# A hybrid decoder layer on one core: the planner's prices, port rule and precedences set anew, and nine products of zeros on TensorE ahead of the first data

## The chip, the core and the metric

The kernel runs on one core of a Trainium2 chip. Five engines work side by side, each through its own list of instructions in a fixed order: TensorE (PE: products, into PSUM), VectorE (DVE), ScalarE (ACT), GpSimd (POOL) and SyncE (SP), which here issues the DMA transfers. An instruction that needs another engine's result waits for a semaphore, and everything behind it on its engine waits too. The metric is the device time of one execution in microseconds (us), lower is better.

## The reference

One step of a decoder layer over a prompt of 1024 tokens and 8 sample tokens, width 1024, all in four-byte floats. The input is projected to 9360 columns (16 of them a low-rank part of the GLA decay). These feed two branches: gated linear attention (GLA, 4 heads, a decay for each key column) and RWKV-7 (16 heads of 64, a delta rule with a 64x64 state). Both are gated, projected up, merged by sigmoid gates, projected out, and normed with the residual. Cut to its core:

```
p = x @ w_in
q, k, v, g_a, a_lr = split(p_gla);  log_a = log_sigmoid(a_lr @ w2 + b) / 16
o_gla = norm(gla_chunked(q, k, v, log_a, S0)) * silu(g_a)
pr = p_rwkv + (prev - p_rwkv) * mu;  r, kb, vb, g_b, w_lr, aa_lr = split(pr)
w = exp(-0.6065 * sigmoid(w0 + tanh(w_lr) @ w2));  a = sigmoid(a0 + aa_lr @ a2)
S_t = S_{t-1} (diag(w_t) - kk_t^T (kk_t * a_t)) + v_t^T k_t;  y_t = S_t r_t
o_rwkv = (groupnorm(y) + bonus) * silu(g_b)
m = sigmoid(gate_a) * (o_gla @ w_up_gla) + sigmoid(gate_b) * (o_rwkv @ w_up_rwkv)
y = layernorm(2**0.25 * x + m @ w_out)
```

The new GLA and RWKV states and the last projected RWKV rows are outputs too.

## The kernel before

**Tiling.** Activations are held transposed, 128 columns of the width on the partitions and tokens along the free dimension. The tokens are run in two passes: 520 (512 of the prompt and the 8 samples), in two tiles of 256 and 264, and then 512. Each of the 73 blocks of 128 output columns is a sum over 8 slabs of the width. To keep four-byte accuracy at TensorE's faster rate, weights and activations are split in a rounded high part and a low rest (`wpart`, `xh`, `xl`), and each slab takes three products: high by high, high by low, low by high. ScalarE makes the high parts (`high`), VectorE or GpSimd the low ones (`low`).

**The two branches.** A GLA head (`gla_head`) runs through seven levels of masked products in halves, then four chunks of 128 tokens. RWKV heads run in pairs (`pair`): `front` makes the scaled keys and queries (tiles `az`, `BK` and `L` in `wide`, `gg`) and solves the inside of each 64-token chunk in 32x32 blocks; the recursion for that (tiles `X`, `Xt`) is 62 small products on GpSimd for each pair. `back` joins the blocks: VectorE transposes `XT` into `Xt`, then TensorE multiplies. `turn` transposes on TensorE, with copies back into `wide`. `chain` carries the state through eight chunks, with a copy of PSUM after each of three products (`pch`), `norm` ends the pair. After the two passes come the up-projections and the output product with the layer norm.

**What sets the order.** Everything is written as generators that yield operations, each a stream. `Order.run` is a planner that runs when the kernel is built: it keeps a model time for each engine and, over and over, issues the ready operation with the lowest key. So the order of every engine's list follows from numbers at the top of the file:

- `price` (L149) gives the model duration of an operation.
[...]
[...]
- `PRIO` and `FOR_PE` are the precedences of the streams, off TensorE and on it; `STAND`, `SCARCE` and `PER_ROW` scale the latter; `URGENT` counts while no weights are ready; `LANDED`, `SWITCH`, `HOLD` and `TABLE` are delays of the model.
- `KEEP` is the number of row buffers that a projected block leaves to others; `EARLY_GATES` is how many saved gate rows are loaded ahead of the last gates of the second pass. With 8, which is their number in each loop, that wait is never reached.

The lines that decide between engines:

```
if eng in op.port:
    free = max(free, self.port["G" if eng == "V" else "V"])
...
end = t + cost
if len(op.ways) > 1:
    end += BIAS if eng == "V" and "A" in op.ways[0][0] else ASIDE if eng == "G" and "G" in op.port else 0.0
```

All operations of the streams are recorded at L221 in the profile, the line of the helper that calls them (L224 after the change), so the tiles tell them apart.

Of the kernel before, what the change touches and what calls it, by code (L numbers as in the profile page):

```python
# [10 lines left out]
F32 = mybir.dt.float32  # L11
# [9 lines left out]
P = 128  # L21
# [32 lines left out]
WBUF = {"wpart": ([P, 2, 512], 4), "wraw": ([P, 512], 3)}  # L54
BANKS = {"proj": 2, "big": 3, "pch": 1, "pY": 2}

KEEP = 3
AHEAD = 3

RAWS = 4  # L60


RANKW, RANKM = 48, 66
SPARE_ROWS = 7
EARLY_GATES = 5


HOP = {"P": 0.2, "D": 0.26, "G": 0.14, "V": 0.14, "A": 0.14}

SWITCH = 0.09  # L70
HOLD = 0.11
TABLE = 1.28

AGE = 0.5

SPARE = 0.4
LANDED = 0.5
BIAS = 0.104
ASIDE = 0.5

PRIO = {"evacuate": 0.7, "pair": 0.3, "turn": 0.5, "chain": 0.5, "norm": 0.1, "x": 0.65, "lora": -0.02, "rank":
        -0.15, "head": 0.3, "gate": -0.18, "w": 0.3, "out": 0.07, "state": 0.16, "block": 0.09}
FOR_PE = {"pair": 1.0, "turn": 1.0, "chain": 1.0, "norm": 1.0, "lora": 1.0, "rank": 1.0, "head": 1.0, "gate": 1.0,
        "state": 1.0, "out": -0.6}
STAND, SCARCE, PER_ROW = 0.017, 0.2, 0.03

URGENT = 0.6
SIGMOID, EXP = "sigmoid_and_others", "natural_log_exp_and_others"
SETS = {AF.Sigmoid: SIGMOID, AF.Tanh: SIGMOID, AF.Exp: EXP, AF.Ln: EXP}

# [14 lines left out]
CST_W = _o  # L105
# [43 lines left out]
def price(eng, name, out, args, ins):  # L149

    n = out.free_size()
    src = [x for x in ins if x.tensor.space != PSUM] if eng == "A" else ins
    if eng == "P":
        m = args[0].free_size()
        rows, cols = tiles(name, args)
        if name == "transpose":
            return 0.112
        if args[0].dtype == F32R:
            return max(m / 1200, n / 2165) if rows == cols == P else (m + n) / 1200
        if rows == cols == P:  # L160
            return 2 * max(m, n) / 1200 + 0.005
        return 2 * (max(m, n) if cols == P else m + n) / 1200 * rows * cols / P ** 2 + (0.01 if cols == P else 0.0)
    if eng == "S":
        return 0.56
    if eng == "A":
        extra = len(ins) - 1
        return 0.097 + n / 1200 + (0.042 if len(src) == len(ins) else 0.0) + 0.094 * extra
    wide = max([n, *(x.free_size() for x in ins)]) if name in ("tensor_reduce", "bn_stats", "bn_aggr") else n
    if eng == "V":
        if name == "tensor_tensor_scan":  # L170
            return 0.1 + n / 480
        if name in ("tensor_copy", "copy", "memset") and ins and ins[0].tensor.space != PSUM:
            wide = wide / 2
        scalars = sum(x.free_size() == 1 for x in ins[1:]) if name in ("scalar_tensor_tensor", "tensor_scalar") else 0
        return 0.068 + wide / (480 if name == "copy_predicated" else 960) + 0.06 * scalars
    if name in ("tensor_scalar", "memset"):
        return 0.08 + n / 760
    return 0.1 + n / (300 if name == "tensor_copy" else 456)


def shared(eng, name, out, ins):

    sb = [x for x in ins if x.tensor.space != PSUM and x.free_size() > 1]
    if eng == "G":
        return bool(sb)
    if name in ("tensor_copy", "copy"):
        return len(sb) > 0 and out.tensor.space != PSUM
    return name in ("tensor_mul", "tensor_add", "tensor_sub", "scalar_tensor_tensor") and len(sb) > 1


# [63 lines left out]
class Order:  # L254
# [83 lines left out]
    def start(self, op):  # L338

        best = None  # L340
        for eng, fn, cost in op.ways:
            free, t = self.time[eng] + (SWITCH if eng == "P" and op.tiles != self.tiles else 0.0), 0.0
            for x in (*op.outs, *op.ins):
# [81 lines left out]
class Kern(Order):  # L425
# [71 lines left out]
    def setup(self):  # L497
        nc, a = self.nc, self.a
        E = mybir.EngineType
        self.es.enter_context(self.tc.manual_schedule(engines={E.PE, E.Activation, E.DVE, E.Pool, E.SP}))  # L500
        cp = self.pool("const")
        wp = self.pool("w", side="left")
        self.dr = self.pool("dr", space=DRAM)
        pp = self.pool("psum", space=PSUM)
        xp = self.pool("x", side="right")
        self.r1 = r1 = self.pool("work", side="left")
        for tag, bufs in BANKS.items():
            self.buffers(tag, bufs, lambda tag=tag, bufs=bufs: pp.tile([P, 512], F32, name=tag, bufs=bufs))
        for tag, (shape, bufs) in SBUF.items():
            dt = F32R if tag in PARTS else F32  # L510
            self.buffers(tag, bufs, lambda tag=tag, shape=shape, bufs=bufs, dt=dt:
                         r1.tile(shape, dt, name=tag, bufs=bufs))
        for tag, (shape, bufs) in WBUF.items():
            dt = F32 if tag == "wraw" else F32R
            self.buffers(tag, bufs, lambda tag=tag, shape=shape, bufs=bufs, dt=dt:
                         wp.tile(shape, dt, name=tag, bufs=bufs))
        for k in range(NK):
            for v in "hl":
                tag = f"x{v}{k}"
                self.buffers(tag, 1, lambda tag=tag: xp.tile([P, HALF], F32R, name=tag, bufs=1))  # L520
        nc.scalar.preload_act_table_set(EXP)
        self.cons = cp.tile([P, CST_W], F32, name="cons")
        self.pv = cp.tile([P, PV_W], F32, name="pv")
        self.ident = self.cst("ident")
        self.omu = cp.tile([P, NRC], F32, name="omu")
        self.oka = cp.tile([P, 8], F32, name="oka")
        self.nkk = cp.tile([P, 8], F32, name="nkk")
        self.bias = {}
        for n, v in [("glaeps", GLA_EPS), ("gneps", GN_EPS), ("lneps", LN_EPS), ("one", 1.0),
                     ("kkl", 0.5 * math.log(KK_SCALE))]:  # L530
            t = cp.tile([P, 1], F32, name="b_" + n)
            nc.vector.memset(t, v)
            self.bias[n] = t
        dbg = getattr(self, "dbg", {})
        self.o_gla = dbg.get("o_gla", None) or self.dr.tile([D, T], F32, name="o_gla")
        self.o_rwkv = dbg.get("o_rwkv", None) or self.dr.tile([D, T], F32, name="o_rwkv")
        self.sg = [[[self.dr.tile([P, PASS[i][1]], F32, name=f"sg{i}{n}{k}") for k in range(NK)] for n in range(2)]
                   for i in range(2)]
        self.mg = [[self.dr.tile([P, PASS[i][1]], F32, name=f"mg{i}{k}") for k in range(NK)] for i in range(2)]

        self.lev = cp.tile([P, 2 * P * MASKED], U8, name="lev")

        self.onesr = cp.tile([P, P], F32R, name="onesr")
        self.headsr = cp.tile([P, P], F32R, name="headsr")
        self.wa = cp.tile([P, NK * RANKW + RANKM - RANKW], F32R, name="wa")
        self.alr = cp.tile([96, HALF], F32R, name="alr")
        self.gw2 = cp.tile([96, GH * GDK], F32R, name="gw2")

        self.GS = [self.dr.tile([P, GDV], F32, name=f"GS{h}") for h in range(GH)]
        self.Sp = [self.dr.tile([P, C], F32, name=f"Sp{n}") for n in range(NPAIR)]  # L550

        self.smp = cp.tile([P, 4, NPAIR, NS], F32, name="smp")
        self.RS = self.dr.tile([4, NS, D], F32, name="RS")
        self.WA = self.dr.tile([2, NS, D], F32, name="WA")
        self.tail = cp.tile([P, NS + 1, NRC], F32, name="tail")
        self.carry = cp.tile([P, NRC], F32, name="carry")
        self.shT = cp.tile([P, NRC, NS], F32, name="shT")
        self.reset = cp.tile([P, HT], U8, name="reset")
        nc.vector.memset(self.reset, 1)
        nc.vector.memset(self.reset[:, ::C], 0)  # L560


        for tag, n, bufs in (("az", 4 * HT, 2), ("XT", 2 * HT, 2), ("L1", HT, 1), ("As", HT, 1)):
            ts = [cp.tile([P, n], F32, name=f"{tag}{i}") for i in range(bufs)]
            for t in ts:
                nc.gpsimd.memset(t, 0.0)
            self.fixed(tag, ts)
# [244 lines left out]
    def gla_row(self, c, rows, scale, paired=None):  # L812
        x = yield from self.row(c.n, KEEP)
        rows.append(x)
# [658 lines left out]
    def gate_row(self, c, n, x):  # L1473
        gt = yield from self.row(c.n, KEEP)

# [313 lines left out]
```

## Time and profile before

| what | value |
|---|---|
| median of 3 runs | 1540.86 us (1540.79 to 1543.17) |
| the profiled execution's own time | 1540.08 us |
| its span, first to last instruction | 1538.3 us |
| granted TensorE clock, mean | 0.997 |
| idle time of TensorE in the span | 29.1 us |
| share of DMA engines in use | 64.8% |

The busy share of TensorE is high from the first weights on: of 31 stretches of 50 us, 28 have it busy for over 48 us. A row of the groups reads: line, engine, operation, output tile <- input tiles, shape, count, then busy time and the mean of one in ns, then the idle time before it with what ended it. A row of the timeline reads: start and length in us, engine, operation, tiles, count, with idle time before it in brackets. A row of the windows reads: stretch, its length, then busy time and count of PE, PEld, DVE, ACT and POOL, the granted clock, the DMA share and GB/s.

### The profile page before, as it was taken

To read this page: it belongs to the slowest core of one execution; us is meant where nothing else is said; L and a number is where in the kernel's file an instruction comes from. 1 tells how busy PE (TensorE), PEld (TensorE's weight loads), DVE (VectorE), ACT (ScalarE), POOL (GpSimd) and SP (SyncE) were. 2 spreads that over 40 slices of the span, in tenths; PEclk is the share of its full clock that TensorE was granted. 3 is DMA by queue.
4 is the path that set the end of the run, shared out by engine and by line. 5 is a ranking of instruction groups with operands and counts; after the bars stand their busy time and mean duration, and the time that the engine had idled before them with its cause. 6 is when DMAs were issued, how large, how long until landed. Compare 5 with 4: busy or idle time off the path is not lost.

```text
span 1538.3 us, 29435 instructions
## 1 busy us (share of the span) xinstructions
PE 1509.2 (98%) x10082; PEld 1347.0 (88%) x10082; DVE 1108.5 (72%) x2324; ACT 837.6 (54%) x2021; POOL 478.1 (31%) x1228
## 2 busy tenths in 40 slices
PE   8999999999999999999999999999999999999998
PEld 8899999999999998888887878787888898897786
DVE  6677687867877796867657796879686856666565
ACT  5556766766566666655545463546556545554210
POOL 1060525042330825073523625451634050000000
PEclk9999999999999999999999999999999999999999
DMA  8777876788568874674565465636574676797432
GB/s 286 266 260 239 269 238 220 225 267 288 192 210 270 280 246 148 215 207 124 161 184 168 122 189 176 179 122 179 178 243 117 222 221 219 265 307 248 137 111 82
DMA packets 206641, 318.44 MB, mean 207 GB/s; under 512 B 87075, under 2 KB 102572, under 8 KB 206492
## 3 DMA queue, kind: packets, MB, share of 16 engines
q1 hardware_dynamic: 206492, 316.56, 64.8%
q8 instruction: 80, 1.31, 0.4%
q14 instruction: 69, 0.57, 0.1%
HBM read 196.82 MB, written 118.61 MB: 205 GB/s over the span
## 4 chain that ended last, share of the span: by engine, by line
PE 79%; DVE 9%; POOL 3%; DMA 3%; issue 2%; ACT 2%; SPq 1%; POOLq 0%; DVEq 0%; ACTq 0%
PE proj L221 47%; PE big L221 19%; PE pY L221 8%; PE pch L221 5%; DVE row L221 4%; POOL X L221 1%; POOL Xt L221 1%; SPq L221 1%; DVE az L221 1%; ACT row L221 1%; DVE part L221 1%; DMA row<-o_gla 1%; DVE wide L221 1%; DVE gg L221 1%; DVE xl L221 1%
## 5 line engine op out<-in xcount | busy, mean ns | idle before, releaser
L221 PE MATMUL proj<-xh,wpart 128*128 128x256 f32 (+2 forms) x3728 | 918.0, 329 | 6.0 <-ACT wpart L221 5.0
L221 PEld LDWEIGHTS proj<-xh,wpart 128*128 128x128 f32 x3728 | 622.8, 189 | 54.5 <-ACT wpart L221 5.0
L221 PE MATMUL proj<-xl,wpart 128*128 128x256 f32 (+2 forms) x1864 | 613.4, 329 | 0.4 <-DVE xl L221 0.4
L221 PEld LDWEIGHTS proj<-xl,wpart 128*128 128x128 f32 x1864 | 352.4, 189 | 21.8 <-DVE xl L221 1.2
L221 POOL TENSOR_TENSOR Xt<-X,wide 128x60 f32<-128x60 f32 (+24 forms) x496 | 166.3, 335 | 223.1 <-DMA wide<-LD 46.5
L221 DVE TENSOR_TENSOR wpart<-wraw,wpart 128x512 fp32r<-128x512 f32 x205 | 143.0, 699 | 70.0 <-ACT wpart L221 64.8
L221 POOL TENSOR_TENSOR X<-X,Xt 128x60 f32<-128x60 f32 (+24 forms) x496 | 172.6, 348 | 38.6
L221 ACT CAST wpart<-wraw 128x512 fp32r<-128x512 f32 x210 | 130.6, 623 | 86.1 <-PE proj L221 41.5
L221 DVE TENSOR_TENSOR row<-row 128x512 f32<-128x512 f32 (+9 forms) x292 | 158.3, 552 | 14.8 <-ACT row L221 8.0
L221 ACT ACTIVATE row<-row 128x512 f32<-128x512 f32 (+3 forms) x229 | 138.2, 611 | 36.0 <-DVE row L221 22.0
L221 POOL TENSOR_TENSOR row<-row 128x256 f32<-128x256 f32 (+6 forms) x77 | 73.3, 957 | 260.4 <-DVE row L221 105.6
L221 ACT ACTIVATE s0p<-wide,pc 64x64 f32<-64x64 f32 x256 | 88.2, 345 | 42.6 <-DVE wide L221 34.4
L221 ACT ACTIVATE row<-proj,omu 128x256 f32<-128x256 f32 (+1 forms) x97 | 53.2, 549 | 86.4 <-PE proj L221 84.5
L221 DVE SCALAR_TENSOR_TENSOR wide<-pch,pc,s0p 64x64 f32<-64x64 f32 x224 | 63.1, 282 | 37.4 <-PE pch L221 32.6
L221 POOL TENSOR_SCALAR XT<-XT,st 128x256 f32<-128x256 f32 x1 | 1.2, 1225 | 272.2 <-ACT st L221 272.2
L221 PE MATMUL big<-row 128*128 128x128 f32 (+3 forms) x456 | 84.2, 314 | 0.0
L221 DVE SCALAR_TENSOR_TENSOR row<-proj,pv,row 128x255 f32<-128x255 f32 (+1 forms) x97 | 55.4, 571 | 29.1 <-ACT tail L221 15.1
L221 PE MATMUL big<-xh,wpart 128*128 128x512 f32 (+2 forms) x304 | 73.3, 325 | 0.0
L221 ACT COPY wide<-pch 64x64 f32<-64x64 f32 x132 | 27.3, 207 | 75.8 <-PE pch L221 51.8
L221 ACT COPY row<-big 128x128 f32<-128x128 f32 (+7 forms) x130 | 39.1, 336 | 53.6 <-PE big L221 49.5
L221 DVE COPY rh<-pch 128x128 f32<-128x128 f32 x128 | 37.1, 290 | 41.8 <-PE pch L221 40.1
L221 ACT ACTIVATE row<-proj 128x128 f32<-128x128 f32 (+4 forms) x136 | 37.2, 326 | 50.9 <-PE proj L221 50.2
(250 smaller groups left out, 2635.5 us busy)
## 6 DMA issues: line engine op xcount, KB each, us to landing
w<-wpart SPq DMA_DIRECT2D x146, 512.0 KB
wpart<-w SPq DMA_DIRECT2D x146, 512.0 KB
wraw<-w_in SPq DMA_DIRECT2D x146, 256.0 KB
wide<-LD SPq DMA_DIRECT2D x64, 128.0 KB
wraw<-w_up_gla SPq DMA_DIRECT2D x32, 256.0 KB
wraw<-w_up_rwkv SPq DMA_DIRECT2D x32, 256.0 KB
sg<-row SPq DMA_DIRECT2D x16, 260.0 KB
row<-sg SPq DMA_DIRECT2D x16, 260.0 KB
```

The lines of the kernel that those rows point to most:

```text
L221: ways.append((eng, lambda call=call: call(out, *args, **kw), price(eng, name, out, args, ins)))
```

## The change

[...] No computation of the layer is changed. The zeros go to the PSUM bank `pch`, whose first later product overwrites them.

```
-KEEP = 3
+KEEP = 2
...
+WARM = 9
-EARLY_GATES = 5
+EARLY_GATES = 8
-SWITCH = 0.09
+SWITCH = 0.074
-LANDED = 0.5
-BIAS = 0.104
-ASIDE = 0.5
+LANDED = 0.605
+BIAS = 0.145
+ASIDE = 1.145
-PRIO = {... "x": 0.65, "lora": -0.02, ... "out": 0.07, ...}
+PRIO = {... "x": 0.56, "lora": 0.08, ... "out": -0.01, ...}
-FOR_PE = {"pair": 1.0, "turn": 1.0, "chain": 1.0, "norm": 1.0, "lora": 1.0, ... "out": -0.6}
+FOR_PE = {"pair": 1.0, "turn": 1.11, "chain": 1.0, "norm": 0.76, "lora": 0.41, ... "out": 0.05}
-STAND, SCARCE, PER_ROW = 0.017, 0.2, 0.03
+STAND, SCARCE, PER_ROW = 0.042, 0.2, 0.036
-URGENT = 0.6
+URGENT = 0.767
...
-            return 0.112
+            return 0.1095
         if args[0].dtype == F32R:
-            return max(m / 1200, n / 2165) if rows == cols == P else (m + n) / 1200
+            return max(m / 1200, 0.0045 + n / 2256) if rows == cols == P else (m + n) / 1200
...
-        extra = len(ins) - 1
+        extra = 0.5 * (len(ins) - 1) if src != ins else len(ins) - 1
...
+    if name in ("tensor_tensor_scan", "tensor_scalar"):
+        return out.free_size() > P and len(sb) > 0
...
+        warm, self.cons = cp.tile([P, P], F32, name="warm"), cp.tile([P, CST_W], F32, name="cons")
+        nc.vector.memset(warm, 0.0)
+        idle = pp.tile([P, 512], F32, name="pch", bufs=BANKS["pch"])
+        for n in range(WARM):
+            nc.tensor.matmul(idle[:, :P], warm, warm, start=True, stop=True)
```

What the numbers do is seen in the engines' lists. TensorE at the very start of the program, before the change (`xh`, `xl` are the first slab's high and low parts):

```order
L1785 UNCONDITIONAL_BRANCH
L221 MATMUL proj<-xh_191,wpart 128x256
L221 MATMUL proj<-xl_196,wpart 128x256
L221 MATMUL proj<-xh_191,wpart 128x256
L221 MATMUL proj<-xh_191,wpart 128x264
```

The same place after it:

```order
L1792 UNCONDITIONAL_BRANCH
L529 MATMUL pch<-warm 128x128 x9
L224 MATMUL proj<-xh_203,wpart 128x256
L224 MATMUL proj<-xl_208,wpart 128x256
L224 MATMUL proj<-xh_203,wpart 128x256
L224 MATMUL proj<-xh_203,wpart 128x264
```

The nine products stand ahead of the first slab; the products behind them are the same.

VectorE early in the first pass, before the change, from the third slab's low part on (`xl_249` is the fifth slab's, `wpart` are halves of weights, `onesr`, `alr` and `wa` are small constants and weights):

```order
L221 TENSOR_TENSOR xl_231<-row,xh_215 128x520
L221 TENSOR_TENSOR xl_242<-row,xh_230 128x520
L221 TENSOR_TENSOR xl_249<-row,xh_241 128x520
L221 MEMSET row 128x520
L221 TENSOR_TENSOR wpart<-wraw,wpart 128x512
L221 CAST onesr<-row 128x128
L221 MEMSET row 128x520
L221 TENSOR_TENSOR wpart<-wraw,wpart 128x512
L221 CAST alr<-row 96x520
L221 CAST wa<-row 128x402
L221 TENSOR_TENSOR xl_304<-row,xh_248 128x520
```

After it (`xl_262` is the fifth slab's):

```order
L224 TENSOR_TENSOR xl_245<-row,xh_227 128x520
L224 TENSOR_TENSOR xl_254<-row,xh_244 128x520
L224 MEMSET row 128x520
L224 CAST onesr<-row 128x128
L224 MEMSET row 128x520
L224 TENSOR_TENSOR wpart<-wraw,wpart 128x512
L224 CAST alr<-row 96x520
L224 CAST wa<-row 128x402
L224 TENSOR_TENSOR wpart<-wraw,wpart 128x512
L224 TENSOR_TENSOR xl_262<-row,xh_253 128x520
L224 TENSOR_TENSOR xl_319<-row,xh_261 128x520
```

The fifth slab's low part has moved behind two halves of weights and the small casts.

GpSimd between the recursions of the last pair of the first pass and the first pair of the second, before the change (`az` and `wide` are the pair's scaled operands, the products on `row` with three dimensions belong to the levels of a GLA head):

```order
L221 MEMSET row 128x8
L221 TENSOR_TENSOR row<-row 128x32x2x4 x2
L221 TENSOR_TENSOR row<-row 128x64
L221 TENSOR_TENSOR az_167<-row 64x8x64 x2
L221 COPY pc<-row 128x8
L221 TENSOR_TENSOR wide<-row 64x8x64
L221 TENSOR_TENSOR row<-row 128x4x2x32 x2
L221 TENSOR_TENSOR row<-row 128x8
L221 MEMSET wide 64x64 x2
L221 TENSOR_TENSOR row<-row 128x2x2x64 x2
L221 TENSOR_TENSOR row<-row 128x512
L221 MEMSET X 128x256
```

After it:

```order
L224 MEMSET row 128x8
L224 TENSOR_TENSOR wide<-row 64x8x64
L224 TENSOR_TENSOR row<-row 128x128x2 x2
L224 TENSOR_TENSOR row<-row 128x64x2x2
L224 TENSOR_TENSOR row<-row 128x128
L224 TENSOR_TENSOR row<-row 128x32x2x4 x2
L224 TENSOR_TENSOR row<-row 128x64
L224 MEMSET X 128x256
```

The two products into `az` and one of 512 columns on `row` are gone from GpSimd, that into `wide` is still there, and some smaller ones of the GLA head have come. Over the whole program, GpSimd's products of 512 or 520 columns (on `row`, `part`, `az`, `wpart` and `wide`) go from 56 to 12, and of the chain's 256 copies `wide<-pch` VectorE keeps 36 of 124 and ScalarE does 220 instead of 132.

More of the change, by code (lines that the diff above doesn't have):

```diff
@@ L76 @@
 SPARE = 0.4
-LANDED = 0.5
-BIAS = 0.104
-ASIDE = 0.5
[L81 to L84, printed above, removed]
-STAND, SCARCE, PER_ROW = 0.017, 0.2, 0.03
-URGENT = 0.6
+LANDED = 0.605
+BIAS = 0.145
+ASIDE = 1.145
+PRIO = {"evacuate": 0.7, "pair": 0.3, "turn": 0.5, "chain": 0.5, "norm": 0.1, "x": 0.56, "lora": 0.08, "rank":
+        -0.15, "head": 0.3, "gate": -0.18, "w": 0.3, "out": -0.01, "state": 0.16, "block": 0.09}
+FOR_PE = {"pair": 1.0, "turn": 1.11, "chain": 1.0, "norm": 0.76, "lora": 0.41, "rank": 1.0, "head": 1.0, "gate": 1.0,
+        "state": 1.0, "out": 0.05}
+STAND, SCARCE, PER_ROW = 0.042, 0.2, 0.036
+URGENT = 0.767
 SIGMOID, EXP = "sigmoid_and_others", "natural_log_exp_and_others"
@@ L156, in price @@
         if name == "transpose":
-            return 0.112
+            return 0.1095
         if args[0].dtype == F32R:
-            return max(m / 1200, n / 2165) if rows == cols == P else (m + n) / 1200
+            return max(m / 1200, 0.0045 + n / 2256) if rows == cols == P else (m + n) / 1200
         if rows == cols == P:
-            return 2 * max(m, n) / 1200 + 0.005
-        return 2 * (max(m, n) if cols == P else m + n) / 1200 * rows * cols / P ** 2 + (0.01 if cols == P else 0.0)
+            return 2 * max(m, n) / 1200 + 0.009
+        return 0.1365 if cols == P else 0.142 if rows == P else 0.95
     if eng == "S":
@@ L521, in setup @@
         nc.scalar.preload_act_table_set(EXP)
-        self.cons = cp.tile([P, CST_W], F32, name="cons")
+        warm, self.cons = cp.tile([P, P], F32, name="warm"), cp.tile([P, CST_W], F32, name="cons")
[3 more added lines that the diff above has]
+            nc.tensor.matmul(idle[:, :P], warm, warm, start=True, stop=True)
         self.pv = cp.tile([P, PV_W], F32, name="pv")
```

## The prediction

> **What bounds the kernel now.** I read the page first, then the waits of TensorE, then the timeline around the longest of them, then the groups of GpSimd.
>
> ```profile
> PE 1509.2 (98%) x10082; PEld 1347.0 (88%) x10082; DVE 1108.5 (72%) x2324; ACT 837.6 (54%) x2021; POOL 478.1 (31%) x1228
> ```
>
> TensorE is busy for 1509.2 of 1538.3 us. The change leaves its products as they are, apart from nine more, so only the 29 us in which it is idle, and stretches at a lower clock, can be won. The waits of TensorE say what that idle time is made of (us in total, times, longest):
>
> ```profile
> PE proj L221 <- ACT wpart L221: 5.0, 1, 5.0
> PE big L221 <- DVE part L221: 3.5, 7, 1.0
> PE big L221 <- DVE Xt L221: 3.4, 4, 1.7
> PE big L221 <- DVE wide L221: 2.0, 1, 2.0
> PE pch L221 <- DVE rh L221: 1.2, 3, 0.7
> PE proj L221 <- DVE row L221: 1.0, 1, 1.0
> ```
>
> ```profile
> 1530.72 0.43 DVE XT L221
> ```
>
> The first 5.0 us are the wait for the first weights. VectorE, though it is idle for 28% of the span, ends nearly all later waits: these five rows of it hold 11.1 us. The last products end at 1530.7 (the row of the chain that ended last), and the 7.6 us behind them hold steps that the change leaves alone. So the question is why VectorE is late at those few places. Two of them:
>
> ```profile
> 625.21 0.68 DVE L221 TENSOR_TENSOR az<-row 64x512 f32<-64x512 f32 x1
> ...
> 694.67 3.26 POOL L221 TENSOR_TENSOR az<-row 64x512 f32<-64x512 f32 x2 [1.46 <-DVE row L221]
> 698.63 1.60 POOL L221 TENSOR_TENSOR wide<-row 64x512 f32<-64x512 f32 x1
> 696.91 1.57 DVE L221 SCALAR_TENSOR_TENSOR row<-row 128x512 f32<-128x512 f32 x1
> 699.01 1.76 DVE L221 TENSOR_TENSOR az<-row 64x512 f32<-64x512 f32 x1
> 700.70 1.24 DVE L221 STREAM_TRANSPOSE Xt<-XT 32x128 f32<-32x128 f32 x4
> 702.00 1.08 PE L221 MATMUL big<-Xt,L 128*128 128x32 f32 x8 [1.70 <-DVE Xt L221]
> ...
> 983.34 2.83 POOL L221 TENSOR_TENSOR row<-row 128x512 f32<-128x512 f32 x2 [10.38 <-DMA row<-state_rwkv]
> 983.59 3.11 DVE L221 COPY gg<-az 64x512 f32<-64x512 f32 x2
> 907.11 0.85 DVE L221 COPY gg<-az 64x512 f32<-64x512 f32 x2
> 987.47 0.66 PE L221 MATMUL big<-cons,row 128*128 128x128 f32 x4 [1.99 <-DVE wide L221]
> ```
>
> The same product of 64x512 takes VectorE 0.68 us at 625.21 and 1.76 us at 699.01, where GpSimd runs a wide product of its own; the two copies into `gg` take 0.85 us alone (907.11) and 3.11 us beside GpSimd (983.59). Each time TensorE waits 1.7 to 2.0 us right behind; the second time for the copy into `wide`, which stands behind those into `gg`. What makes VectorE late is wide work on GpSimd at the same moment.
>
> **The change, part by part.** Its own time is 1540.08 us in the profiled execution (span 1538.3 and 1.8 around it), 0.05% below the median of 1540.86; the sum is made against 1540.08.
>
> (1) Wide products leave GpSimd. `ASIDE` more than doubles, and the port list grows. What GpSimd ran of 512 columns and more:
>
> ```profile
> L221 POOL TENSOR_TENSOR row<-row 128x512 f32<-128x512 f32 x23 | 32.3, 1408 | 113.3 <-DVE row L221 54.7 <-DMA row<-state_rwkv 26.5 <-ACT row L221 17.3
> L221 POOL TENSOR_TENSOR part<-row,part 128x512 fp32r<-128x512 f32 x12 | 17.1, 1429 | 71.9 <-ACT part L221 31.9 <-DVE part L221 28.8 <-PE big L221 11.2
> L221 POOL TENSOR_TENSOR row<-row 128x520 f32<-128x520 f32 x7 | 9.8, 1396 | 39.1 <-ACT row L221 39.1
> L221 POOL TENSOR_TENSOR az<-row 64x512 f32<-64x512 f32 x6 | 8.3, 1388 | 23.5 <-ACT row L221 13.6 <-issue 8.4 <-DVE row L221 1.5
> L221 POOL TENSOR_TENSOR wpart<-wraw,wpart 128x512 fp32r<-128x512 f32 x5 | 6.7, 1343 | 123.9 <-DMA wide<-LD 73.3 <-PE proj L221 25.9 <-ACT wpart L221 24.8
> L221 POOL TENSOR_TENSOR wide<-row 64x512 f32<-64x512 f32 x3 | 4.5, 1501 | 19.7 <-DVE row L221 19.6
> ```
>
> That is 56; the changed order leaves 12 of these kinds on GpSimd, none of `part` and none of `az`. The waits I lay to such meetings are those on `part`, `Xt` and `wide`, 3.5 + 3.4 + 2.0 = 8.9 us. After the wait of 1.70 us there is a price on top:
>
> ```profile
> 703.94 0.63 PE L221 MATMUL proj<-xl,wpart 128*128 128x512 f32 x1
> 703.23 0.39 PE L221 MATMUL proj<-xl,wpart 128*128 128x512 f32 x1
> 704.00:707.40 3.40, 3.40 (x14) 2.94 (x12) 3.35 (x8) 0.18 (x1) 0.00 (x0) 0.52 0.13 10
> ```
>
> The granted clock is 0.52 for 3.4 us, and a 512-column product takes 0.63 instead of 0.39. Five such products at 0.43 instead of 0.23 us from start to start cost 1.0 us. So 9.9 us hang on it. With 12 of the 56 left I take three quarters, **-7.4 us**; the bounds are 0 (each wait is dealt out anew elsewhere) and -12.1 (all 11.1 us of waits on VectorE and the clock).
>
> (2) The price of that: 44 products more on VectorE, 0.68 us each, 30 us. It gets back the chain's copies:
>
> ```profile
> L221 DVE COPY wide<-pch 64x64 f32<-64x64 f32 x124 | 27.4, 221 | 50.0 <-PE pch L221 45.8 <-ACT sto L221 1.1 <-ACT row L221 1.0
> L221 ACT COPY wide<-pch 64x64 f32<-64x64 f32 x132 | 27.3, 207 | 75.8 <-PE pch L221 51.8 <-DVE wide L221 22.2
> ```
>
> 88 of the 124 go to ScalarE, which is no slower at them (207 against 221 ns) and busy for 54%; VectorE loses 19 us. With some 0.9 us saved at each meeting that no longer happens, VectorE's busy time stays near 1108. In a stretch where it is fuller than on average, TensorE still does not wait:
>
> ```profile
> 200.00:250.00 50.00, 50.00 (x426) 49.13 (x425) 43.38 (x93) 33.62 (x94) 14.56 (x35) 1.00 0.71 228
> ```
>
> VectorE is busy for 43.38 of 50 us and TensorE for all 50. So most of the 44 are covered. But some now stand ahead of a step that TensorE waits for: I take **+2 us**, three or four of 0.6 us; the bounds are 0 and, with no cover at all, +30.
>
> (3) The nine products of zeros. Before:
>
> ```profile
> 7.58 0.58 PE L221 MATMUL pY<-xh,wpart 128*128 128x256 f32 x1 [0.58 <-ACT wpart L221]
> 8.31 0.80 PE L221 MATMUL pY<-xh,wpart 128*128 128x256 f32 x2
> 10.86 0.34 PE L221 MATMUL pY<-xl,wpart 128*128 128x256 f32 x1
> 11.40 0.28 PE L221 MATMUL pY<-xh,wpart 128*128 128x264 f32 x1
> 11.52 0.28 PE L221 MATMUL proj<-xh,wpart 128*128 128x256 f32 x1
> 8.36 2.04 DVE L221 TENSOR_TENSOR xl<-row,xh 128x520 fp32r<-128x520 f32 x3
> 10.46 0.49 DVE L221 MEMSET row<- 128x520 f32 x1
> 13.36 0.69 DVE L221 TENSOR_TENSOR xl<-row,xh 128x520 fp32r<-128x520 f32 x1
> ```
>
> From 8.31 to 10.86 eleven products start 0.23 us apart; from 11.40 on it is 0.12. At full pace these eleven take 1.3 instead of 2.55 us. Up to 8.3 the pace does not matter, since TensorE waits for weights there (7.58). Zeros can start once VectorE has cleared their tile, near 1.2 us (an estimate), and are 18 passes. The row at 702.00 holds eight such passes of four products, 1.08 us with the drain of the last, some 0.11 us each; at half the clock 18 of them are 4 us, and they end near 5.1, where the first real product starts (5.02). Then VectorE must keep up: the fifth slab's low part now stands behind two weight halves and the small casts. Those took 10.46 to 13.36 before; from 9.7, when two low parts are done, they end at 12.6, and that slab is ready at 13.3. TensorE wants it near 13.2. So -1.25 + 0.1 = **-1.1 us**; the bounds are +0.3 (no faster clock, and the zeros in the way) and -1.3.
>
> [...]
>
> (4) Other numbers (`KEEP`, `EARLY_GATES`, prices, precedences) move products among each other. The number of changes between full-rate and four-byte products on TensorE grows by some 45; at these changes the first starts later by what the last started earlier, so I take +0.5 in all, bounds -2 and +3.
>
> Sum: -7.4 + 2 - 1.1 + 0.5 = -6.0, and 1540.08 - 6.0 = **1534.1 us**.
>
> **Rivals.**
> (a) *All waits on VectorE shrink*, since the whole order fits better: -12.1 - 1.1 and no price, 1527. For it: nearly every row of waits names VectorE. Against: 12 wide products stay on GpSimd.
>
> (b) *Waits are only dealt anew.* Every engine has an order of its own, and moving 44 products shifts when all others come; the lost waits return on other rows. Then only the zeros and +0.5 remain: 1539.5. For it: 98% leaves little, and the waits are few and scattered.
>
> (c) *Slower: VectorE as the bound in front of the transposes into `Xt`.* The 44 products are 2.75 for each of 16 head pairs; inline, at some 0.61 us from start to start (0.68 less the overlap of two), they put those transposes, and the product that waits for them, 1.7 us later. Where TensorE has nothing else, it pays. Against the 8.0 us won by (1), (3) and (4) it decides from five pairs on; with nine it gives 1540.1 - 8.0 + 15.3 = 1547.4. Against it: the stretch with 43.38 above.
>
> (d) *The zeros wake nothing*: term (3) is 0 to +0.3, 1535.3.
>
> [...]
>
> ```profile
> L221 POOL TENSOR_TENSOR Xt<-X,wide 128x60 f32<-128x60 f32 (+24 forms) x496 | 166.3, 335 | 223.1 <-DMA wide<-LD 46.5
> ```
>
> **How the numbers follow.** The forecast as it stands 0.39, (d) 0.12, (a) 0.17, (b) 0.20, (c) 0.12. A measurement of this kernel tells about 0.2%, 3.1 us, from no change: faster is below 1537.8, slower above 1543.9. The forecast, (d) and (a) make 0.68, all faster but for 0.02 of (d) that lies above 1537.8: 0.66; (b) and that part 0.22; slower 0.12. The range goes from a little below (a), for waits that the rows above leave out, to the near end of (c): 1526 to 1543.
>
> **What would show it.** Right: GpSimd's wide groups at 12 in all, `gg` copies and `az` products at their undisturbed length, no wait over 1.5 us on `Xt` or `wide`, no half clock in mid-span, 0.12 us pace from 8.3 us on, VectorE's busy time near 1108. Wrong: `part` and `Xt` still lead the waits with more than 6 us together, or new rows of VectorE or ScalarE carry as much.

## The result, and the profile after

| | before | after |
|---|---|---|
| median | 1540.82 us (1540.38 to 1543.17) | 1521.02 us (1520.08 to 1524.11) |
| ratio, 95% interval | | 0.9872 (0.9855 to 0.9889) |
| profiled execution, its span | 1540.08, 1538.3 us | 1520.7, 1518.9 us |
| granted clock, mean | 0.997 | 0.999 |

The kernel is 1.28% faster, 19.8 us where 6.0 were forecast: the right direction, but below the range's lower end of 1526. From the page of the changed kernel, busy time, share of the span and instructions:

```profile
PE 1502.7 (99%) x10100; PEld 1348.3 (89%) x10100; DVE 1092.3 (72%) x2306; ACT 853.0 (56%) x2107; POOL 395.1 (26%) x1161
```

And TensorE's waits (us in total, times, longest):

```profile
PE big L224 <- issue: 1.7, 1, 1.7
PE pch L529 <- DVE warm L526: 1.0, 1, 1.0
PE proj L224 <- DVE row L224: 1.0, 1, 1.0
...
PE big L224 <- DVE part L224: 0.6, 2, 0.3
PE pch L224 <- DVE rh L224: 0.6, 1, 0.6
```

The waits on `part` fell from 3.5 to 0.6 us, those on `wide` are gone, and of `Xt` one is left (the first row, see below). Where the time went is seen by stage. The rows of the windows give stretch and length, then busy time of PE, PEld, DVE, ACT and POOL with counts, clock, DMA share and GB/s. Before:

```profile
50.00:600.00 550.00, 547.13 (x4535) 529.34 (x4534) 417.43 (x899) 351.23 (x922) 203.33 (x516) 1.00 0.75 242
600.00:1200.00 600.00, 590.32 (x3313) 491.64 (x3311) 446.32 (x962) 323.66 (x769) 242.62 (x627) 1.00 0.57 170
1200.00:1420.00 220.00, 217.65 (x1417) 195.25 (x1416) 144.02 (x283) 115.07 (x226) 21.71 (x66) 1.00 0.78 251
```

And after:

```profile
50.00:600.00 550.00, 549.12 (x4565) 531.75 (x4564) 418.66 (x914) 355.94 (x953) 177.28 (x504) 1.00 0.73 243
600.00:1200.00 600.00, 597.37 (x3404) 503.78 (x3403) 446.92 (x970) 345.34 (x848) 186.47 (x575) 1.00 0.59 180
1200.00:1420.00 220.00, 217.57 (x1372) 194.17 (x1371) 136.12 (x254) 111.90 (x214) 20.89 (x62) 1.00 0.75 240
```

From 600 to 1200 us, most of the second pass, TensorE starts 91 more products in the same time. That stage is where most of the gain is; from 1200 on nothing is won.

Idle time understates it: a product is still busy when the next one starts (0.28 us long, 0.12 us from start to start, for 264 columns), so a product that comes late by less than this overlap leaves no gap. So I also took **lateness** from the trace: the distance from one product's start to the next, less the median distance of the same form of product in the trace of before, summed by stage, in us (so products packed more tightly than the median count below zero). "Met" counts VectorE's instructions that took over 0.1 us longer than the undisturbed median of their form while GpSimd worked on something other than the recursion. "Chain" is where the last product of the last head pair's chain starts. Each row is one profiled execution, and stretches at half clock count in its lateness (13.7 us of half clock in the second pass of nudge_before, 20.5 us from 1200 to 1400 in port_alone and in nudge_after3). Behind 1400 another 3.2 us stand in port_alone, 7.2 in precedences_undone and 8.2 in nudge_after3, and under 1 in the others. The experiments stand in the table too:

| kernel | ratio to before | 0-50 | 50-600 | 600-1200 | 1200-1400 | met | chain |
|---|---|---|---|---|---|---|---|
| before | 1 | 5.1 | 8.7 | 15.7 | 4.5 | 48 | 1332 |
| **after** | 0.9872 | 4.0 | 4.1 | 0.8 | 5.7 | 12 | 1316 |
| zeros_alone | 0.9991 | 5.2 | 10.7 | 16.3 | 4.2 | 49 | 1334 |
| port_alone | 1.0114 | 4.5 | 10.5 | 9.4 | 23.2 | 21 | 1370 |
| moved | 1.0003 | 4.5 | 9.8 | 15.8 | 5.1 | 9 | 1333 |
| nudge_before | 1.0004 | 5.0 | 9.0 | 20.7 | 5.6 | 43 | 1338 |
| nudge_before2 | 1.0016 | 5.4 | 9.4 | 15.6 | 5.7 | 48 | 1329 |
| port_undone | 1.0013 | 5.1 | 12.7 | 15.3 | 8.7 | 47 | 1350 |
| aside_back | 1.0003 | 4.3 | 11.7 | 13.7 | 5.7 | 43 | 1320 |
| rule_out | 1.0043 | 3.8 | 18.3 | 7.0 | 13.9 | 22 | 1361 |
| prices_undone | 0.9965 | 6.7 | 6.4 | 8.4 | 12.5 | 18 | 1327 |
| precedences_undone | 1.0025 | 3.5 | 5.3 | 10.4 | 12.7 | 19 | 1354 |
| buffers_undone | 0.9946 | 3.9 | 9.8 | 8.3 | 4.8 | 11 | 1324 |
| zeros_undone | 0.9892 | 5.2 | 4.3 | 1.2 | 7.3 | 13 | 1320 |
| back | 0.9935 | 4.2 | 4.8 | 5.4 | 12.5 | 37 | 1328 |
| nudge_after | 0.9906 | 3.8 | 3.9 | 1.4 | 10.6 | 13 | 1311 |
| nudge_after2 | 0.9883 | 4.8 | 5.0 | 3.8 | 7.7 | 14 | 1322 |
| nudge_after3 | 1.0107 | 5.3 | 5.6 | 7.0 | 29.2 | 14 | 1369 |

From before to after the lateness falls by 19.3 us, from 34.0 to 14.7, which is the difference of the spans but for 0.1. Behind waits that the profile shows it falls by 12.3 (23.3 to 11.0, of which rows of idle time show 16.5 and 7.5); the start gives 1.3; the half-clock stretch of before 1.5 (the prediction's 1.0 for five products leaves out the short ones behind them); the other 4.2 are products that come closer without any wait shown.

Two places that the prediction named. The start after the change:

```profile
1.04 4.21 PE L529 MATMUL pch<-warm 128*128 128x128 f32 x18 [1.04 <-DVE warm L526]
4.91 0.58 PE L224 MATMUL proj<-xh,wpart 128*128 128x256 f32 x1
...
8.44 0.29 PE L224 MATMUL pY<-xh,wpart 128*128 128x264 f32 x1
8.57 0.28 PE L224 MATMUL proj<-xh,wpart 128*128 128x256 f32 x1
...
22.56 0.28 PE L224 MATMUL big<-xl,wa 128*66 128x264 f32 x1
```

```profile
23.81 0.28 PE L221 MATMUL big<-xl,wa 128*66 128x264 f32 x1
```

Products start 0.13 us apart at 8.44, and the one that started at 23.81 before (second fence) starts at 22.56: 1.25 us, as forecast. The other place is the wait for `Xt`, from the timeline after the change:

```profile
679.07 1.58 POOL L224 TENSOR_TENSOR wide<-row 64x512 f32<-64x512 f32 x1 [10.97 <-DVE row L224]
679.42 3.05 DVE L224 TENSOR_TENSOR az<-row 64x512 f32<-64x512 f32 x2
685.13 0.92 DVE L224 STREAM_TRANSPOSE Xt<-XT 32x128 f32<-32x128 f32 x3
686.47 1.05 PE L224 MATMUL big<-Xt,L 128*128 128x32 f32 x8 [1.70 <-issue]
```

And the window behind it, in the columns of the windows above:

```profile
686.40:689.80 3.40, 3.33 (x21) 3.00 (x21) 3.31 (x7) 1.14 (x5) 0.00 (x0) 1.00 0.13 48
```

The product into `wide` that stayed on GpSimd still meets those into `az` (3.05 us for two), and TensorE waits the same 1.70 us. But no half clock follows: 1.00 was granted in the 3.4 us behind.

### The profile page after: what moved, and what is told of

Its sections match the earlier page's. It is cut to its first block, busy times and chain, and to the rows that moved or that the text cites. A ratio compares the mean times of both kernels' runs of the same rounds, so it can differ in the third digit from the quotient of the medians.

```text
span 1518.9 us, 29410 instructions
## 1 busy us (share of the span) xinstructions
PE 1502.7 (99%) x10100; PEld 1348.3 (89%) x10100; DVE 1092.3 (72%) x2306; ACT 853.0 (56%) x2107; POOL 395.1 (26%) x1161
## 4 chain that ended last, share of the span: by engine, by line
PE 94%; DVE 3%; DMA 1%; issue 1%; ACT 0%; SPq 0%; POOL 0%; POOLq 0%; DVEq 0%; ACTq 0%
PE proj L224 58%; PE big L224 21%; PE pY L224 9%; PE pch L224 6%; DVE row L224 1%; DMA wide<-LD 0%; DMA row<-o_gla 0%; DVE wide L224 0%; DVE wpart L224 0%; DVE xl L224 0%; DMA wraw<-w_in 0%; SPq L224 0%; DVE part L224 0%; ACT xh L224 0%; DVE pc L224 0%
## 5 line engine op out<-in xcount | busy, mean ns | idle before, releaser
L224 PE MATMUL proj<-xh,wpart 128*128 128x264 f32 (+2 forms) x3728 | 918.3, 329 | 1.0 <-DVE row L224 1.0
L224 PE MATMUL proj<-xl,wpart 128*128 128x264 f32 (+2 forms) x1864 | 614.5, 330 | 0.4 <-DVE xl L224 0.4
L224 DVE TENSOR_TENSOR row<-row 128x512 f32<-128x512 f32 (+10 forms) x331 | 173.3, 533 | 8.0 <-ACT row L224 2.2
L224 POOL TENSOR_TENSOR X<-X,Xt 128x60 f32<-128x60 f32 (+24 forms) x496 | 162.6, 328 | 38.8
L224 ACT ACTIVATE row<-row 128x512 f32<-128x512 f32 (+4 forms) x229 | 138.5, 612 | 29.0 <-DVE row L224 19.6
L224 ACT COPY wide<-pch 64x64 f32<-64x64 f32 x220 | 45.6, 207 | 107.3 <-PE pch L224 103.7
L224 POOL TENSOR_TENSOR row<-row 128x256 f32<-128x256 f32 (+4 forms) x38 | 36.3, 961 | 266.6 <-DVE row L224 187.6
L224 PE MATMUL big<-xh,wpart 128*128 128x256 f32 (+2 forms) x304 | 73.7, 327 | 0.6 <-ACT xh L224 0.6
L224 PEld LDWEIGHTS big<-row 128*128 128x128 f32 (+2 forms) x456 | 58.8, 176 | 5.0 <-ACT row L224 0.6
```

What stands on the lines that cost most here:

```text
L224: ways.append((eng, lambda call=call: call(out, *args, **kw), price(eng, name, out, args, ins)))
```

## The experiments

Two theories. **Meetings**, the prediction's term (1): what costs is VectorE's work stretched beside wide products of GpSimd, so kernels without them should gain whatever else they do. **The order**: what costs is where the planner puts each operation, its numbers work as a set, and the meetings are worth little by themselves. And the zeros apart.

### One part alone, and the parts undone

**zeros_alone**: the change's block of zeros in the kernel before.

```
+        for n in range(WARM):
+            nc.tensor.matmul(idle[:, :P], warm, warm, start=True, stop=True)
```

> The kernel before with the nine products of zeros alone, all numbers of the planner as before. Port theory (the gain in mid-program comes from GpSimd's wide products leaving): 1.3 us faster, 1539.5, with the wait of the first blocks near 23.8 us in the old trace moved to 22.6 and nothing else changed. A rival by which the earlier start lets transfers run ahead and so shortens later waits too: over 4 us faster.

0.9991 (0.9976 to 1.0006): 1.3 us can't be told from nothing here. The profile tells more. Two windows of zeros_alone, then the same two of after:

```profile
4.40:7.80 3.40, 2.11 (x12) 1.35 (x10) 2.25 (x4) 1.96 (x4) 3.23 (x10) 0.95 0.98 336
7.80:11.20 3.40, 3.33 (x17) 3.19 (x17) 2.92 (x6) 2.69 (x5) 0.59 (x2) 0.55 1.02 398
```

```profile
4.40:7.80 3.40, 2.98 (x13) 2.24 (x11) 2.30 (x4) 2.26 (x4) 3.23 (x10) 1.00 1.01 364
7.80:11.20 3.40, 3.22 (x26) 3.22 (x27) 3.13 (x7) 2.56 (x5) 0.60 (x2) 1.00 1.05 411
```

The timeline names the wait, zeros_alone first, then after:

```profile
7.28 0.45 PE L222 MATMUL pY<-xh,wpart 128*128 128x256 f32 x1 [1.06 <-ACT wpart L222]
```

```profile
7.25 0.39 PE L224 MATMUL pY<-xh,wpart 128*128 128x256 f32 x1 [0.38 <-ACT wpart L224]
```

In zeros_alone the wait for weights ahead of 7.28 is 1.06 us long (0.38 in after), and the clock behind it is 0.55 from 7.80 to 11.20. The wait alone doesn't explain it, since it is partly the work of a full pace that came earlier. The 18 passes of zeros take 4.21 us in after and start 0.21 us apart from the second on. In zeros_alone they take 3.70; 17 of them have started by 4.40 us, in after 15:

```profile
1.04 3.70 PE L527 MATMUL pch<-warm 128*128 128x128 f32 x18 [1.04 <-DVE warm L524]
```

In after full pace comes only near 7 us (the clock of 1.00 in its first row above stands there for want of a record: products still take 0.42 us up to 6.45, and 0.28 from 7.48 on), so TensorE reaches the late weights later and waits less. Of the twelve profiled executions with zeros seven keep the full clock behind 7.8 us (1.00), five lose it (0.50 to 0.55 from 7.80 to 11.20: zeros_alone, port_undone, prices_undone, nudge_after2, nudge_after3). The zeros and their start, at 1.04, are the same in after and zeros_alone, so the same instructions met full pace at different times. TensorE's busy time in the stretch before doesn't decide it alone: buffers_undone keeps the clock with 2.37 us busy from 4.40 to 7.80, nudge_after2 loses it with 2.38. Nor does the wait for the late weights, 1.0 us in buffers_undone and 0.5 in nudge_after2.

**zeros_undone**: the changed kernel without that block; the rest of its order is the same row for row.

```
-        for n in range(WARM):
-            nc.tensor.matmul(idle[:, :P], warm, warm, start=True, stop=True)
```

> The kernel after without the zeros; the order of every engine is else the same row for row. Every theory so far: 1.3 us slower than after, 1522.3, with half pace up to about 11 us. Rival: the lead of 1.3 us is lost in later waits, and the two are the same, 1521.0.

0.9892 (0.9871 to 0.9913), 3.1 us above the changed kernel's ratio, with intervals that overlap: 1.3 fits, and so does 0. Its profile has the product of 22.56 some 1.3 us later, and a stretch of 3.4 us at a clock of 0.50 from 1216.7 on, which the changed kernel's profile doesn't have.

**port_alone**: only `ASIDE` and the longer port list, in the kernel before. The port list is `shared`, a rule of the planner: its model runs the operations on it one at a time, whether on VectorE or on GpSimd. Where an operation can go to either, `ASIDE` is the handicap on GpSimd for those on the list; `BIAS` is that on VectorE against ScalarE. Whether the chip runs them one at a time no run shows; what it does where the two meet is counted as "met" above.

```
-ASIDE = 0.5
+ASIDE = 1.145
...
+    if name in ("tensor_tensor_scan", "tensor_scalar"):
+        return out.free_size() > P and len(sb) > 0
```

> The kernel before with ASIDE at 1.145 and scan and tensor_scalar on the port list, nothing else: 22 of 58 wide products stay on GpSimd. Port theory: most of the 18.5 us that the change brings besides the zeros, that is 10 to 16 us faster (1525 to 1531), slowed VectorE operations falling from 48 to under 20. Rival (precedences and prices carry it, the port little): within 4 us of before.

**Slower**, 1.0114 (1.0070 to 1.0158), by 18 us. Two windows:

```profile
600.00:1200.00 600.00, 592.93 (x3305) 494.17 (x3304) 438.43 (x972) 325.47 (x751) 198.55 (x559) 1.00 0.59 175
1200.00:1420.00 220.00, 206.31 (x1343) 186.18 (x1342) 143.15 (x280) 121.84 (x242) 54.23 (x129) 0.95 0.71 223
```

And its waits:

```profile
PE big L223 <- ACT xh L223: 3.2, 2, 3.0
PE big L223 <- DMA XT<-XD: 2.9, 1, 2.9
PE big L223 <- ACT As L223: 2.8, 2, 2.5
```

In the second pass TensorE is late by 9.4 instead of 15.7 us, 6.3 less, near the 7.4 of term (1). But from 1200 to 1400 it is late by 23.2 instead of 4.5. About 12 of that stand between 1240 and 1280, where TensorE's list has it wait for the steps that join one of the last two head pairs, and where the clock falls to 0.51 from 1256 to 1270:

```profile
1257.33 1.89 PE L223 MATMUL big<-Xt,L 128*128 128x32 f32 x8 [2.94 <-DMA XT<-XD]
1261.69 1.97 PE L223 MATMUL big<-XT,As 128*128 128x64 f32 x8 [2.48 <-ACT As L223]
```

The last head pair's chain ends 38 us later than before, and near 1398 TensorE waits 3.0 us for the input of the last up-projection (`xh`).

**port_undone**: the reverse, the changed kernel with those two edits taken back. **aside_back** takes back only `ASIDE`, **rule_out** only the port list.

```
-ASIDE = 1.145
+ASIDE = 0.5
...
-    if name in ("tensor_tensor_scan", "tensor_scalar"):
-        return out.free_size() > P and len(sb) > 0
```

> The kernel after with ASIDE at 0.5 and the old port list: 53 wide products on GpSimd again. Port theory: 10 to 16 us of the 19.8 are lost, 1531 to 1537. Rival (precedences and prices): under 5 us lost, below 1526.

> The kernel after with ASIDE at 0.5, the longer port list kept, so that GpSimd gets wide products again. Theory of work late against the plan: most of what the undone port lost is lost here too, 10 to 22 us, 1531 to 1543, and the second pass is where. Rival (the rule is enough, since the plan then knows all meetings): under 6 us lost.

> The kernel after without the two new kinds on the port list, ASIDE kept at 1.145. With so few wide products left on GpSimd the list has little to say: by the theory of work that is late against the plan, the second pass keeps most of its gain, and 2 to 8 us are lost by the new dealing, 1522 to 1529. Rival (the rule is what sets the order right): 12 us or more lost.

1.0013 (0.9995 to 1.0031), 1.0003 (0.9992 to 1.0014) and 1.0043 (1.0028 to 1.0057): each alone takes back the whole gain or more. With `ASIDE` at 0.5 the second pass is as late as before (15.3, 13.7); without the list alone it is not (7.0), but the first pass is (18.3). The waits, rule_out first, then aside_back:

```profile
PE proj L222 <- ACT xh L222: 4.8, 2, 3.6
PE big L222 <- DVE S L222: 3.5, 5, 1.1
```

```profile
PE big L224 <- DVE part L224: 4.4, 8, 0.9
```

In aside_back `part` leads again as before the change. That rule_out would lose 26 us I had not expected.

**prices_undone**, **precedences_undone**, **buffers_undone**: one group of term (4) each taken back in the changed kernel.

```
-SWITCH = 0.074
-LANDED = 0.605
-BIAS = 0.145
+SWITCH = 0.09
+LANDED = 0.5
+BIAS = 0.104
...
```

with the old `price`;

```
-STAND, SCARCE, PER_ROW = 0.042, 0.2, 0.036
+STAND, SCARCE, PER_ROW = 0.017, 0.2, 0.03
-URGENT = 0.767
+URGENT = 0.6
...
```

with the old `PRIO` and `FOR_PE`; and

```
-KEEP = 2
+KEEP = 3
-EARLY_GATES = 8
+EARLY_GATES = 5
```

> The kernel after with the old prices and delays of the model (price, SWITCH, LANDED, BIAS), all else of the change kept. The first two theories fell with the port runs; now three are held. Dealing theory (the numbers are one set; any set deals about the same work in another order, and how well the waits fall is a property of the set, not of one number): 5 to 25 us slower than after, 1526 to 1546, whichever group is undone. Price theory (the new prices bring the gain): this one loses over 12 us, the other groups under 5. Precedence theory: under 5 us lost here.

> The kernel after with the old precedences (PRIO, FOR_PE, STAND and its scale, URGENT), all else kept. Dealing theory: 5 to 25 us slower than after, 1526 to 1546. Precedence theory: over 12 us lost here and under 5 in the other groups. Price theory: under 5 lost here.

> The kernel after with KEEP 3 and EARLY_GATES 5 again, all else kept. Dealing theory: 3 to 20 us slower than after. Price and precedence theories: within 4 us of after, 1517 to 1525.

0.9965 (0.9949 to 0.9980), 1.0025 (1.0014 to 1.0035) and 0.9946 (0.9924 to 0.9967). Against 0.9872, taking them back costs 14, 24 and 11 us, and port_undone 22. Together that is 71 us, of a gain of 19.8: the groups don't add. What one of them is worth depends on the others.

### Do the meetings cost?

**moved**: the plan of before is kept, and TensorE's list with it; only where a product of 512 columns or more stands on GpSimd, VectorE issues it at that place (58 products).

```
-            op.fn()
+            other = {e: f for e, f, _ in op.ways}
+            aside = op.eng == "G" and "V" in other and op.out.free_size() >= 512 and op.ins
+            (other["V"] if aside else op.fn)()
```

> The kernel before with its plan kept, so that every other instruction stands where it stood; but the 58 wide products that the plan gives to GpSimd are issued on VectorE at the same place. Port theory: VectorE gains 39 us of work and loses some 34 us of slowing, waits on part, Xt and wide fall by more than half, 5 to 10 us faster (1531 to 1536). Rival (work inline on VectorE costs what meetings cost): within 3 us of before or slower.

1.0003 (0.9987 to 1.0018). The meetings fall from 48 to 9, and nothing is won. Its waits:

```profile
PE big L221 <- DVE part L221: 6.6, 14, 0.8
...
PE pch L221 <- DVE rh L221: 1.6, 3, 1.1
PE big L221 <- DVE Xt L221: 1.4, 3, 0.7
```

`wide` is gone and `Xt` halved, but `part` has gone from 3.5 to 6.6. The page of moved has VectorE busy for 1114.3 us with 2382 instructions, that of before for 1108.5 with 2324: the 58 products, some 39 us of work, come in place of nearly as much stretching. So moved trades one for the other at the same place; it doesn't take the meetings away for nothing. That is the prediction's rival (b), the waits dealt out anew.

**back**: the reverse. The changed plan is kept, TensorE's list too, and every 13th wide product that VectorE or GpSimd could do is issued on GpSimd (49).

```
-            op.fn()
+            other = {e: f for e, f, _ in op.ways}
+            back = op.eng == "V" and "G" in other and op.out.free_size() >= 512 and op.ins
+            self.count = getattr(self, "count", 0) + (1 if back else 0)
+            (other["G"] if back and self.count % 13 == 0 else op.fn)()
```

> The kernel after with its plan kept and TensorE's order the same row for row, but every 13th wide product that could run on either engine (49 in all) is issued on GpSimd at the same place. The theory now: what costs is work on VectorE that comes later than the plan has it, by a meeting with GpSimd or by work inline that the plan does not know of; in the second pass (600 to 1200 us) that cost 14.9 of the 19.8 us. It expects meetings to return in tens, TensorE to wait on VectorE again in that stretch, and 6 to 15 us lost, 1527 to 1536. Rival (the moved-run has shown that meetings as such cost nothing, only the new order of TensorE gains): within 3 us of after.

0.9935 (0.9916 to 0.9953), 9.7 us lost, with 37 meetings instead of 12. Its waits:

```profile
PE big L224 <- issue: 2.8, 1, 2.8
PE proj L224 <- ACT xh L224: 2.5, 1, 2.5
PE pch L224 <- ACT wide L224: 1.8, 1, 1.8
```

So wide work on GpSimd that the plan doesn't know of does cost. But moved shows that work which the plan has on GpSimd costs as much when VectorE does it at that place. What both may have in common is that a result comes later than the plan has it; no run isolates that. Neither tells the stretching apart from the GpSimd product's own 1.4 us against 0.7.

### How steep is the ground?

**nudge_after**, **nudge_after2**, **nudge_after3**: one number of the changed kernel moved by 3 to 8%. **nudge_before** and **nudge_before2** do it in the kernel before, by 10 and 6%.

```
-ASIDE = 1.145
+ASIDE = 1.05
```

```
-BIAS = 0.145
+BIAS = 0.15
```

```
-STAND, SCARCE, PER_ROW = 0.042, 0.2, 0.036
+STAND, SCARCE, PER_ROW = 0.045, 0.2, 0.036
```

```
-ASIDE = 0.5
+ASIDE = 0.55
```

```
-BIAS = 0.104
+BIAS = 0.11
```

> The kernel after with one number moved by 8%, ASIDE 1.05 for 1.145, which gives GpSimd hardly more wide work. Dealing theory: the order of the engines changes throughout, and 2 to 15 us are lost, though no cost of the hardware has changed. Price and precedence theories, and any by which a nameable cost was removed: within 3 us of after, 1518 to 1524.

> The kernel after with BIAS 0.15 for 0.145, nothing else. Fitted-set theory (the set of after is a point picked out of many dealings, its neighbours deal like the rest): 2 to 12 us slower than after. Rival (the numbers are right in themselves, and neighbours are as good): within 2.5 us of after, either way.

> The kernel after with STAND 0.045 for 0.042, nothing else. Fitted-set theory: 2 to 12 us slower than after. Rival: within 2.5 us of after, either way.

> The kernel before with ASIDE 0.55 for 0.5, nothing else. Fitted-set theory, if the set of before was such a point too: 2 to 12 us slower than before. Rival (before lies anywhere among its neighbours): faster as likely as slower.

> The kernel before with BIAS 0.11 for 0.104, nothing else. Fitted-set theory: 2 to 12 us slower than before. Rival: faster as likely as slower. In all four, and by every theory that the earlier runs left: TensorE's lateness in the second pass stays near 15 us with ASIDE at 0.5 and below 7 us with ASIDE at 1.145.

0.9906 (0.9880 to 0.9931), 0.9883 (0.9868 to 0.9897), **1.0107** (1.0092 to 1.0122), 1.0004 (0.9994 to 1.0014) and 1.0016 (1.0007 to 1.0026). The neighbours of before cost 0.6 and 2.5 us; those of after 5, 2 (not told from nothing) and 36. Of the 41 us by which the profiled execution of nudge_after3 is longer than that of after, 23.5 stand between 1200 and 1400, 7.9 behind and 6.2 in the second pass. The longest wait, which with the half clock behind it makes 12.7 us of lateness from 1380 to 1400, is seen in its chain (start, length, what):

```profile
1388.96 5.00 DMA row<-o_rwkv
1393.98 0.63 ACT xh L224
1394.60 0.04 issue
1394.65 5.36 PE big L224 x11
```

In its timeline, the product that waits:

```profile
1394.65 0.79 PE L224 MATMUL big<-xh,wpart 128*128 128x512 f32 x1 [8.28 <-ACT xh L224]
```

And in two windows, while it waits and behind:

```profile
1386.00:1394.60 8.60, 0.36 (x3) 0.15 (x2) 3.21 (x6) 2.48 (x4) 0.00 (x0) 0.76 0.93 290
1395.00:1398.40 3.40, 3.40 (x8) 2.45 (x8) 2.78 (x5) 2.71 (x5) 0.00 (x0) 0.50 1.05 402
```

The last pair's chain ends at 1369 instead of 1316. From there its output goes to memory, is loaded back (5.00 us), is split, and only then can the last up-projection start. TensorE has nothing left at 1386.4, waits 8.28 us, and runs at half the clock behind. In the changed kernel the timeline has the last output's store (1335.30), its reload in parts, and the split into high parts, for which TensorE waits 0.6 us in all; nudge_after3 stores it at 1385.91 (second fence):

```profile
1335.30 0.32 SPq L224 DMA_DIRECT2D o_rwkv<-row  x1
1348.46 1.81 SPq L224 DMA_DIRECT2D row<-o_rwkv  x2
1362.85 2.18 ACT L224 CAST xh<-row 128x512 fp32r<-128x512 f32 x4 [2.05 <-PE big L224]
```

```profile
1385.91 0.32 SPq L224 DMA_DIRECT2D o_rwkv<-row  x1
```

In the three kernels with the chain's end at 1361 or later (port_alone, rule_out, nudge_after3) this stage is late by 13.9 to 29.2 us; in the others by 4.2 to 12.7. Among those the two don't go together: nudge_after ends its chain first of all, at 1311, and is late by 10.6.

## Why the prediction was right or wrong

**(1), -7.4 for wide products that leave GpSimd.** The count was right (12 left), and so was the place: second-pass waits on `part`, `wide` and `Xt` behind `ASIDE`. All kernels with `ASIDE` near 0.5 are late by 13.7 to 20.7 us there, all others by 0.8 to 10.4. The reason isn't borne out. moved does what the term asks for, wide products from GpSimd to VectorE, with the order held, and wins nothing: the -7.4, less the +2 of term (2), was not to be had from that alone. The step "what makes VectorE late is wide work on GpSimd at the same moment" took what stood beside the wait for all of its cause. Whether the meetings cost something that the same work in line on VectorE takes up again is not told. The two edits pay where the planner deals out the whole order by them, 6.3 us in that stage in port_alone.

**(2), +2 for work on VectorE.** Nothing like it is seen: VectorE is busy for 1092.3, not 1108, and its rows of waits shrank. Nor do the recursion's small products on GpSimd (the prediction's row of 496, 335 ns each) hold VectorE up much: in the changed kernel's trace the 56 products into `wpart` on VectorE that met the recursion alone took 0.72 us on the mean and the 142 undisturbed ones 0.69, 0.03 us each.

**(3), -1.1 for the zeros.** Measured in the profile as -1.25. That zeros bring full pace forward was the author's estimate; in after it came near 7.0 us, in before near 11.0. Rival (d) came true elsewhere, though: with the same zeros, five of twelve profiled executions lost the clock again and got nothing or little (they are late by 4.8 to 6.7 us up to 50 us, the kernels without zeros by 4.5 to 5.4, the other seven by 3.5 to 4.3). That the profile of the changed kernel is one of the seven is luck as far as the runs show. What decides between the two kinds no run shows: 2.37 us busy kept the clock, 2.38 lost it, and the same zeros met full pace at different passes.

**(4), +0.5 for all other numbers, bounds -2 and +3. This step failed.** It took prices, precedences and buffers for small things because no row of the trace names them, and gave them a term of their own to be added to (1). Without the port edits the term holds: port_undone, the zeros and all the other numbers alone, is 2 us slower than before. On top of the port edits it does not: from port_alone, 18 us slower, to the changed kernel, 20 faster, is 37 us, of which the zeros are 1.25 by the profile. So these numbers are worth about 36 us there, where -2 was the bound, and taking back any one group of them costs 11 to 24. It is the sum of separate terms that fails. By the table the groups' loss stands in the second pass (7.5 to 9.6 us more than in after), for prices and precedences also from 1200 to 1400 (7 us), for buffers in the first pass (5.7).

**The pool was too small as well.** The prediction let only idle rows count, 11.1 us for VectorE. Behind all waits after the first product 23.3 us of lateness stood, where rows of idle time show 16.5, since each hides the overlap with the product ahead; 12.3 of them were won. The 4.2 us without a wait came with TensorE's new order: lateness without a shown wait is 10.8 us in before and 11.3 in moved, which keeps its list; in zeros_undone, which has the new one, it is 7.0.

**The rivals.** (a), all waits shrink since the order fits better, was the closest in kind; its 1527 had the same small pool. (b) is what moved does. (c), slower, came in port_alone, but mostly at the end of the second pass: its waits on the transposes into `Xt` are 1.3 us. The signs: wide groups at 12, no half clock in mid-span, full pace from 8.4 and `part` under 6 us came as said; one `Xt` wait over 1.5 us stayed, two `az` products beside GpSimd still took 3.05 us, and VectorE's busy time fell below 1108.

**Open:** which property of the new order wins the second pass, and which numbers bring it. The runs that take numbers back deal out the whole order anew, so none isolates one. That the changed point was picked from many is suggested by its steep neighbours and not shown.

## What to carry to other kernels

Where a planner sets the order, its numbers are one set: judge them by the whole and by their neighbours, and test a suspected cause with the order held fixed, as moved and back do. An operation that stands beside a wait is a suspect only. Look at the last serial hand-over (last pair, store, reload, split), since what is won earlier can be lost there, as in nudge_after3 and, by the pair before it too, in port_alone.

## What the runs showed of the hardware

- A wait of the same length led to half the clock in one kernel and not in another: 1.70 us at 702.0 in before, with 3.4 us at 0.52 behind it, and 1.70 us at 686.5 in after, with 1.00. In before the longer wait, 1.99 us at 987.5, had 1.00 behind it too. The traces' clock records change at 10.98, 703.88, 707.30 and 1533.32 us in before and at 7.01 and 1515.70 in after, and each distance within a trace is a multiple of 3.413 us.
- With nine four-byte products of zeros ahead (18 passes from 1.04 us) full pace came near 7.0 us in after, against 11.0 in before, and earlier in zeros_alone (17 passes started by 4.40 us instead of 15). In five of twelve executions with zeros it was lost again from 7.80 to 11.20 (0.50 to 0.55), behind waits for weights of 0.5 to 1.2 us; buffers_undone kept it behind one of 1.0.
- In after products of 256 columns of the split parts start 0.118 us apart, and an unsplit four-byte one of 128 columns takes two passes some 0.11 us apart. Behind such passes the first product of split parts starts after 0.03 us, and the one after it 0.08 us later than usual (0.316 instead of 0.232 for 512 columns). So at the changes of term (4) the two shifts cancel.
- VectorE's stretching beside wide GpSimd work is large (a product into `az` 1.76 us instead of 0.68 in before, 3.05 us for two in after), yet removing 39 of 48 such meetings, by VectorE doing GpSimd's wide products at the same places, moved the time by 0.03%, within the interval.
